# A gated convolution's input projection: one block group more, four plain column tiles fewer, operands taken unscaled

## The chip, the cores and the metric

One core of one Trainium2 chip. The metric is device time in microseconds (us), lower is better. The engines are TensorE (PE; its weight loads are PEld), VectorE (DVE), ScalarE (ACT), GpSimd (POOL) and SyncE (SP); SP and POOL mostly issue DMAs here.

## What is computed

A two-layer decoder trunk on x of 512 tokens by 1024 features: attention, a gated MLP, a short-convolution mixer, a gated MLP, each behind an RMS norm and added to the residual h. The change lies in the mixer:

```python
def short_conv_mixer(h, norm_g, w_in, conv_w, w_out):
    xn = rms_norm(h, norm_g)
    proj = xn @ w_in                      # 1024 -> 3072 columns
    gate_b, gate_c, u = proj[..., :1024], proj[..., 1024:2048], proj[..., 2048:]
    y = gate_b * causal_dwconv(gate_c * u, conv_w)   # width 3 along the tokens
    return y @ w_out
```

The norm is a gain per feature and one factor r per token (a row, since features lie on partitions and tokens along the free side). As r is a factor of each token, it can be applied to the input or to each projected column: `gate_c * u` then owes r twice, `gate_b` once.

## The kernel before, in words

All matrix products are in float32 split in two (high and low half, `whi`/`wlo` for weights, `hi`/`lo` for operands): three matmuls per product, high by high, high by low, low by high. ScalarE writes a high half, VectorE the low half (L1027 and L1029 in `halves_to`, L315 and L316 for plain weight tiles).

*Plain tiles.* A tile is 128 of the 3072 output columns: eight blocks of 128 input features, three matmuls of 512 tokens each, 24 matmuls (`products`, L336 to L338). They read `hs_a`/`hs_b`, halves of h times gain, unscaled by r, which the end of the first MLP writes (L372, L373). What comes out is multiplied by r.

*Block groups.* `Sevens` computes four tiles (two column tiles of one part by two of another) in seven products instead of eight: input features and tokens are cut in halves, and seven sums of quarters (forms p1, p7, p3, p6, p2, q5, q4) meet seven sums of weight blocks. A product is 24 matmuls of 256 tokens (`seven`, L1078); a group has 168. The forms are made once for all groups. The weight sums are made for each group: X and Y are loaded by SP (L1093, L1094), then Y += a block by a DMA of POOL (L1105), Y += X on VectorE (L1144), X += a block by a DMA of POOL (L1105), Y += W on VectorE (L1199); W and Z are loaded (L1102). Halves of each sum follow in `weights_of`. Halves of weights have three buffers, which plain tiles share. `slot(g, s)` writes out the order by hand: seven slots a group, each with its product (slot 2 has p3 of the group before) and the vector and scalar work around it.

The 24 column tiles of the mixer's projection are done as eight plain tiles (two of u, two of gate_c, the first four of gate_b) and four groups: groups 1 to 3 are two tiles of u and two of gate_c each, group 4 the last four tiles of gate_b. During the plain tiles the chore `prepare` makes x = h times gain times r (eight operations, L1453) and from it all seven forms (L1459, L1029), so that the groups' results need no r. `input_` (L1467, L1469, L446) does the two plain tiles of u and gate_c, `gate` (L1475) scales a tile of gate_b. `conv` is a scaled copy on ScalarE (L443) and two operations on VectorE (L446). `times` (L1404) multiplies by gate_b; group 4 does that in place. `halves_in` makes y's halves, which the out-projection (eight plain tiles, from 736.4 us) reads.

Order on an engine is the program's order as a scheduler with a cost model rearranges it, before the run; `pin` keeps an instruction in program order, `behind(a, b)` puts a behind b on its engine. Each engine and each DMA queue then takes its list in order.

Of the kernel before, what the change touches and what calls it, by code (L numbers as in the profile page):

```python
# [17 lines left out]
F32 = mybir.dt.float32  # L18
# [4 lines left out]
ALU = mybir.AluOpType  # L23
# [34 lines left out]
def trunk(  # L58
# [153 lines left out]
    def conv_tap(j, t):  # L212
        i = 24 + j * 8 + t
        return gains[:, i:i + 1]
# [51 lines left out]
    def want(dram, k0, nk, c0, n, *more):  # L266
        wanted.append((dram, k0, nk, (c0, n) + more))
# [173 lines left out]
    def causal_conv(dst, src, tap):  # L441

        act.activation(dst, src, AF.Copy, scale=tap(2))  # L443
        for j in (1, 0):
            d = 2 - j
            dve.scalar_tensor_tensor(dst[:, d:], src[:, 0:S - d], tap(j), dst[:, d:], op0=ALU.mult, op1=ALU.add)  # L446


    w_in, w_out = attn_w_in[0], attn_w_out[0]
# [36 lines left out]
    GROUPS = ((0, 2), (2, 2), (4, 2), (6, 1), (7, 2), (9, 2))  # L486

    def want_conv():
        for part, o in ((2, 0), (1, 0), (2, 1), (1, 1)) + tuple((0, o) for o in range(4)):
            want(conv_w_in[0], 0, 8, part * D + o * P, P)  # L490

    def want_conv_out():
        for o in range(ND):
# [532 lines left out]
    def halves_to(hi, lo, src, sign=1.0, held=()):  # L1026
        made = act.activation(hi, src, AF.Copy, scale=sign)  # L1027
        if sign > 0:
            rest = dve.tensor_tensor(lo, src, f32(hi), op=ALU.subtract)  # L1029
        else:  # L1030
            rest = dve.scalar_tensor_tensor(lo, src, -1.0, f32(hi), op0=ALU.mult, op1=ALU.subtract)
        for m, engine in ((made, "act"), (rest, "dve")):
            if engine in held:
                pin(m)

    LEFT, RIGHT = slice(0, HT), slice(HT, S)
    FORMS = ("p1", "p7", "p3", "p6", "p2", "q5", "q4")
# [45 lines left out]
    class Sevens:  # L1083
# [23 lines left out]
        def weights_of(self, g, form, n):  # L1107
            hi, lo = (wp.tile([P, CHUNK], F32R, tag=f"w{t}", name=f"w{t}_{form}{self.name}{g}", bufs=3)[:, 0:1024].rearrange(
                "p (k c) -> p k c", c=2 * P) for t in ("hi", "lo"))
            halves_to(hi, lo, self.st[g][n], held=("act",))  # L1110
            self.st[g][form] = hi, lo

        def bank_of(self, g, n):
# [16 lines left out]

        def join(self, g, n, acc, other):
            to = self.wides[g][n][:, :, RIGHT]
            dve.tensor_tensor(to, acc.rearrange("p (i t) -> p i t", t=HT), other.rearrange("p (i t) -> p i t", t=HT), op=ALU.subtract)
            if self.scaled:
                dve.tensor_tensor(to, to, self.row(RIGHT), op=ALU.mult)

# [4 lines left out]
        def first_sums(self, g):  # L1141
            self.weights_of(g, "p7", "Y")
            if not self.table:
                dve.tensor_tensor(self.st[g]["Y"], self.st[g]["Y"], self.st[g]["X"], op=ALU.add)  # L1144
            self.add_block(g, "X", 0, 1)
            if self.table:
                self.load_one(g, "three", self.table("6", g))
# [143 lines left out]
    class RawForms:  # L1291
# [9 lines left out]
        def make(self, name, k=slice(0, 4)):  # L1301
            (a, b), (c, d) = ((x[:, k, LEFT], x[:, k, RIGHT]) for x in self.x)
            s0, s1 = (t[:, k, :] for t in self.s)
            src, made = {
                "p1": (a, None), "p7": (s0, (a, b, ALU.subtract)), "p6": (s0, (s0, d, ALU.add)), "p2": (c, None),
                "q5": (s1, (b, d, ALU.subtract)), "q4": (d, None), "p3": (s0, (c, s0, ALU.subtract))}[name]
            if made:
                dve.tensor_tensor(src, made[0], made[1], op=made[2])
            halves_to(*(t[:, k, :] for t in self.up.forms[name]), src)

    def up_seven(layer, norm, mp):
        blocks, up = up_begin(layer, norm, mp, mp)
# [55 lines left out]
    def conv_seven(norm, mp, rp):  # L1368
# [2 lines left out]
            c0 = (4 + 2 * half) * P if g == 4 else (2 - half) * D + 2 * g * P  # L1371
            return conv_w_in[0][kh * 512:(kh + 1) * 512, c0:c0 + 2 * P].rearrange("(k p) c -> p k c", p=P)

        up = Sevens("c", mp, range(1, 5), block_of)
        up.norm, up.chores, up.ahead = norm, [], True
        chores, wides, room = up.chores, up.wides, []

        def eight(dt, name):
            t = rp.tile([P, 8, S], dt, tag="head", name=name)
            return t[:, 0:4, :], t[:, 4:8, :]  # L1380
        early_t, early_b = eight(F32, "early")
        ys = []

        def place(k, n):
            if not room:
                room.append(hsp.tile([P, 12, S], F32, tag="hs_a", name="hs_a_conv"))
            return room[0][:, k:k + n, :]
        up.wides_of = lambda g: {"yg": place(8, 2), "yv": place(10, 2)}

        def conv(o, src):  # L1390
            dst = early_t[:, 2 + o, :] if o < 2 else place(o, 1)[:, 0, :]
            causal_conv(dst, src, lambda i: conv_tap(i, o))

        def halves_in(o, n):
# [6 lines left out]

        def times(o, side, with_):
            t = place(o, 2)[:, :, side]
            dve.tensor_tensor(t, t, with_, op=ALU.mult)  # L1404

        def by_tile(acc):
            return acc.rearrange("p (i t) -> p i t", t=HT)
# [15 lines left out]
        def tail(p, s):  # L1423
            u, c = (wides[p][n] for n in ("yg", "yv"))
            if p == 4:
                if s == 0:
                    open_ys()
                    times(6, RIGHT, c[:, :, RIGHT])
                    times(4, RIGHT, u[:, :, RIGHT])
                    halves_in(4, 2)  # L1430
                elif s == 3:
                    halves_in(6, 2)
            elif s == 0:
                if p == 2:
                    halves_in(2, 2)
            elif s == 1:
                dve.tensor_tensor(u[:, :, RIGHT], u[:, :, RIGHT], c[:, :, RIGHT], op=ALU.mult)
            elif s in (3, 4):
                conv(2 * p + s - 3, u[:, s - 3, :])
            elif s == 5 and p == 1:  # L1440
                dve.tensor_tensor(place(0, 2), early_t[:, 2:4, :], early_b[:, 0:2, :], op=ALU.mult)
                times(2, slice(0, S), early_b[:, 2:4, :])
                open_ys()
            elif s == 6 and p == 1:
                halves_in(0, 2)
        up.tail = tail

        def prepare():
            x0, x1 = mp.tile([P, 4, S], F32, tag="x0", name="x0_prep"), rp.tile([P, 4, S], F32, tag="four", name="x1_prep")
            s0, s1 = (mp.tile([P, 4, HT], F32, tag=t, name=f"{t}_prep", bufs=2) for t in "XY")  # L1450
            for x, f in ((x0, 0), (x1, 4)):
                for i in range(4):
                    dve.scalar_tensor_tensor(x[:, i, :], h[:, f + i, :], gain_of(norm.base, f + i), norm.row, op0=ALU.mult, op1=ALU.mult)  # L1453
                    yield 0.75
            a, b, c, d = x0[:, :, LEFT], x0[:, :, RIGHT], x1[:, :, LEFT], x1[:, :, RIGHT]
            for n, src, made in (("p1", a, None), ("p7", s0, (a, b, ALU.subtract)), ("p6", s0, (s0, d, ALU.add)), ("p2", c, None),
                                 ("q5", s1, (b, d, ALU.subtract)), ("q4", d, None), ("p3", s0, (c, s0, ALU.subtract))):
                if made:
                    dve.tensor_tensor(src, made[0], made[1], op=made[2])  # L1459
                    yield 1.22  # L1460
                halves_to(*up.forms[n], src)
                yield 1.22

        def input_(o, u, c):
            x, y = early_t[:, 0, :], early_t[:, 1, :]
            for t, acc in ((x, u), (y, c)):
                dve.tensor_tensor(t, acc, norm.row, op=ALU.mult)  # L1467
                yield 0.69
            dve.tensor_tensor(x, x, y, op=ALU.mult)  # L1469
            yield 0.69  # L1470
            conv(o, x)
            yield 1.5

        def gate(o, acc):
            dve.tensor_tensor(early_b[:, o, :], acc, norm.row, op=ALU.mult)  # L1475
            yield 0.69

        accs = []
        for j in range(8):
            accs.append(bank("bbbbaabb"[j]))  # L1480
            for _ in products(accs[-1], weights(), (4, 5, 6, 7, 0, 1, 2, 3)):
                up.work_off(SHARE)
            if j in (1, 3):
                chores.append(input_(j // 2, *accs[j - 1:]))
            if j == 3:
                chores.append(prepare())
            if j >= 4:
                chores.insert(0, gate(j - 4, accs[j]))
            if j == 5:
                up.load_pair(1)  # L1490
                up.add_block(1, "Y", 1, 1)
            if j == 7:
                up.weights_of(1, "p1", "X")
                up.first_sums(1)
                up.weights_of(1, "p6", "Y")
        want_conv_out()
        for s in range(28):
            up.slot(1 + s // 7, s % 7)
            if s == 20:
                sum_far(99)  # L1500
            if s == 27:
                fetch(1)
        for s in (0, 2, 3):
            up.slot(5, s)
# [287 lines left out]
```

## Time and profile before

| | us |
|---|---|
| three runs | 1117.97, 1118.03, 1118.71 (median 1118.03) |
| profiled execution | 1119.06 |
| its span, first to last instruction | 1117.3 |
| plain tiles of the projection | 610.2 to 656.3 |
| four block groups | 656.3 to 736.4 |
| out-projection | 736.4 to 781.1 |

The granted TensorE clock is 1.00 of full speed in all stretches shown, its level of 2.4 GHz. An engine's busy time is the time in which it has an instruction under way; matmuls overlap, so a busy TensorE tells nothing of its rate, and a delay is read from the length of a run of equal matmuls.

### The profile page before, as it was taken

What the parts mean: (1) busy time and instruction counts of PE and PEld (TensorE: products, weight loads), DVE (VectorE), ACT (ScalarE), POOL (GpSimd) and SP (SyncE); (2) the same over time, 40 slices, a digit from 0 to 9 for tenths busy, and PEclk for the clock granted to TensorE, in tenths of its full rate; (3) what the DMA queues carried; (4) which work ended last, traced back from release to release, by engine and by line L of the source; (5) the groups of instructions that cost most, each with busy time, mean ns of one, the idle gap of its engine ahead of it and who ended that gap; (6) DMA issues with size and microseconds to landing.
All of it is one profiled execution on the core that took longest, in us unless ns stands there. A gap on an engine that the chain in (4) does not pass through costs nothing.

```text
span 1117.3 us, 19714 instructions
## 1 busy us (share of the span) xinstructions
PE 1109.9 (99%) x7803; PEld 1014.2 (91%) x7803; DVE 960.8 (86%) x1483; ACT 681.2 (61%) x1006; POOL 175.4 (16%) x199
## 2 busy tenths in 40 slices
PE   9999999999999999999999999999999999999998
PEld 7888787878899999999999899988999999998886
DVE  6798888997899787898989888867899999999886
ACT  7466677655466666666557355545666656567553
POOL 4011111111012221014400001110111221014300
PEclk9999999999999999999999999999999999999999
DMA  6668877778678887899963355696879887899951
GB/s 196 169 182 202 199 175 207 190 206 227 177 174 200 204 202 177 218 271 193 226 178 81 113 145 139 138 278 168 214 185 219 195 201 181 218 260 206 231 152 57
DMA packets 176988, 210.94 MB, mean 189 GB/s; under 512 B 7580, under 2 KB 142796, under 8 KB 176896
## 3 DMA queue, kind: packets, MB, share of 16 engines
q0 software_dynamic: 50112, 92.19, 42.7%
q1 hardware_dynamic: 126624, 117.42, 33.4%
q8 instruction: 61, 1.00, 0.3%
q14 instruction: 31, 0.25, 0.1%
q10 hardware_dynamic: 160, 0.07, 0.0%
HBM read 204.68 MB, written 44.04 MB: 223 GB/s over the span
## 4 chain that ended last, share of the span: by engine, by line
PE 96%; DVE 2%; issue 1%; ACT 1%; DVEq 0%; ACTq 0%
PE psb L1078 31%; PE psa L1078 12%; PE psb L1670 11%; PE psa L1670 8%; PE psb L336 6%; PE psb L338 5%; PE psb L337 5%; PE psb L710 2%; PE psa L338 2%; PE psa L337 2%; PE psa L336 2%; PE psa L807 2%; PE psc L782 1%; PE psb L592 1%; PE psb L593 1%; PE psb L594 1%
## 5 line engine op out<-in xcount | busy, mean ns | idle before, releaser
L1078 PE MATMUL psb<-p_hi,whi_p 128*128 128x256 f32 x480 | 135.4, 282 | 0.0
L1078 PE MATMUL psb<-p_lo,whi_p 128*128 128x256 f32 x480 | 135.2, 282 | 0.0
L1078 PE MATMUL psb<-p_hi,wlo_p 128*128 128x256 f32 x480 | 135.0, 282 | 0.0
L315 ACT ACTIVATE whi<-raw 128x1024 fp32r<-128x1024 f32 (+2 forms) x81 | 83.2, 1028 | 80.3 <-PE psb L337 27.8
L316 DVE TENSOR_TENSOR wlo<-raw,whi 128x1024 fp32r<-128x1024 f32 (+2 forms) x81 | 95.8, 1183 | 20.8 <-ACT whi L315 20.2
L1078 PEld LDWEIGHTS psb<-p_hi,whi_p 128*128 128x128 f32 x480 | 91.0, 189 | 0.0
L1078 PEld LDWEIGHTS psb<-p_lo,whi_p 128*128 128x128 f32 x480 | 90.5, 189 | 0.0
L1078 PE MATMUL psa<-p_hi,wlo_p 128*128 128x256 f32 x320 | 90.2, 282 | 0.0
L1078 PE MATMUL psa<-p_lo,whi_p 128*128 128x256 f32 x320 | 90.2, 282 | 0.0
L1078 PE MATMUL psb<-q_lo,whi_q 128*128 128x256 f32 x320 | 90.2, 282 | 0.0
L1078 PE MATMUL psb<-q_hi,whi_q 128*128 128x256 f32 x320 | 90.1, 282 | 0.0
L1078 PEld LDWEIGHTS psb<-p_hi,wlo_p 128*128 128x128 f32 x480 | 90.1, 188 | 0.0
L1078 PE MATMUL psa<-p_hi,whi_p 128*128 128x256 f32 x320 | 90.0, 281 | 0.0
L1078 PE MATMUL psb<-q_hi,wlo_q 128*128 128x256 f32 x320 | 90.0, 282 | 0.0
L336 PE MATMUL psb<-hs_a,whi 128*128 128x512 f32 x192 | 79.3, 413 | 0.0
L338 PE MATMUL psb<-hs_a,wlo 128*128 128x512 f32 x192 | 76.2, 398 | 0.0
L1670 PE MATMUL psb<-act,whi 128*128 128x256 f32 x352 | 63.3, 282 | 0.0
L1078 PEld LDWEIGHTS psa<-p_hi,whi_p 128*128 128x128 f32 x320 | 60.6, 190 | 0.1
L1078 PEld LDWEIGHTS psb<-q_hi,whi_q 128*128 128x128 f32 x320 | 60.6, 189 | 0.0
L1078 PEld LDWEIGHTS psa<-p_lo,whi_p 128*128 128x128 f32 x320 | 60.3, 189 | 0.1
L1078 PEld LDWEIGHTS psb<-q_lo,whi_q 128*128 128x128 f32 x320 | 60.4, 189 | 0.0
L1078 PEld LDWEIGHTS psa<-p_hi,wlo_p 128*128 128x128 f32 x320 | 60.1, 188 | 0.0
(551 smaller groups left out, 3596.7 us busy)
## 6 DMA issues: line engine op xcount, KB each, us to landing
t<-in_ffn_w_up POOLq DMA_DIRECT2D x24, 768.0 KB, 8.0
raw<-in_attn_w_in SPq DMA_DIRECT2D x24, 512.0 KB, 5.0
t<-in_ffn_w_up POOLq DMA_DIRECT2D x12, 1024.0 KB, 10.1
X<-in_ffn_w_up SPq DMA_DIRECT2D x20, 512.0 KB, 5.0
Y<-t SPq DMA_DIRECT2D x20, 512.0 KB, 6.6
three<-t SPq DMA_DIRECT2D x20, 512.0 KB, 5.4
W<-in_ffn_w_up SPq DMA_DIRECT2D x20, 512.0 KB, 4.0
Z<-in_ffn_w_up SPq DMA_DIRECT2D x20, 512.0 KB, 5.5
```

The lines of the kernel that those rows point to most:

```text
L315: return (act.activation(hi[:, at_], raw[:, at_], AF.Copy), dve.tensor_tensor(lo[:, at_], raw[:, at_], f32(hi[:, at_]), op=ALU.subtract))
L316: dve.tensor_tensor(lo[:, at_], raw[:, at_], f32(hi[:, at_]), op=ALU.subtract))
L336: made = [pe.matmul(acc, w[0], rhs[0], start=first, stop=False), pe.matmul(acc, w[0], rhs[1], start=False, stop=False), pe.matmul(acc, w[1 ...
L337: pe.matmul(acc, w[0], rhs[1], start=False, stop=False),
L338: pe.matmul(acc, w[1], rhs[0], start=False, stop=last)]
L592: pe.matmul(acc, lhs[0], w[0], start=first, stop=False)
L593: pe.matmul(acc, lhs[0], w[1], start=False, stop=False)
L594: pe.matmul(acc, lhs[1], w[0], start=False, stop=last)
L710: pe.matmul(ss[e][:, c:c + wide], ql[rows, b * P:n], kl[rows, 0:wide], start=first and b == bs[0], stop=last and b == bs[-1])
L807: pe.matmul(out_, w, t[:, first:first + step * (NB - k - 1) + 1:step, :], start=k == 0 and i == 0, stop=k == NB - 1 and i == 1)
L1078: pe.matmul(to, w[a][:, k, c], x[b][:, k, :], start=fresh and i + k + t == 0, stop=i == 1 and k == 3 and t == 2, skip_group_check=not fresh)
L1670: pe.matmul(to, l, r, start=begin and o + t == 0, stop=end and t == 2 and o == (0 if layer else 1), skip_group_check=not fresh)
```

## The change

Five groups and four plain tiles (the first four of gate_b). Group 0 takes the first two tiles of u and of gate_c. The forms are now sums of h times gain, without r, as the plain operands are: p1, p2 and q4 are plain quarters, which DMAs of POOL's queue copy from `hs_a`/`hs_b` (six copies, high and low half, 512 KB each); p7, p6, q5 and p3 are made by `RawForms` from eight copies on ScalarE (`raw.take`). So u times gate_c is multiplied by r squared (`row2`) in each of groups 0 to 3, and tiles 4 to 7 of the convolved product by r in two more products, since group 4's gate has no r either. Five vector operations are put behind others with `behind`: gate 3, q5's difference, p3's difference, the two products with r, and the convolution of tile 7 (six calls, the two products in one kind). The scratch of p7, p6 and q5 moves from X's and Y's buffers to `early`.

```diff
     def want_conv():
-        for part, o in ((2, 0), (1, 0), (2, 1), (1, 1)) + tuple((0, o) for o in range(4)):
-            want(conv_w_in[0], 0, 8, part * D + o * P, P)
+        for o in range(4):
+            want(conv_w_in[0], 0, 8, o * P, P)
...
-        up = Sevens("c", mp, range(1, 5), block_of)
+        up = Sevens("c", mp, range(5), block_of)
...
         def conv(o, src):
-            dst = early_t[:, 2 + o, :] if o < 2 else place(o, 1)[:, 0, :]
-            causal_conv(dst, src, lambda i: conv_tap(i, o))
+            return causal_conv(place(o, 1)[:, 0, :], src, lambda i: conv_tap(i, o))
...
             if p == 4:
                 if s == 0:
                     open_ys()
-                    times(6, RIGHT, c[:, :, RIGHT])
                     times(4, RIGHT, u[:, :, RIGHT])
                     halves_in(4, 2)
+                    behind(times(6, slice(0, S), both(norm.row)), up.joined)
+                    times(6, RIGHT, c[:, :, RIGHT])
...
             elif s == 1:
                 dve.tensor_tensor(u[:, :, RIGHT], u[:, :, RIGHT], c[:, :, RIGHT], op=ALU.mult)
+                if p == 3:
+                    behind(times(4, slice(0, S), both(norm.row)), up.rest)
             elif s in (3, 4):
-                conv(2 * p + s - 3, u[:, s - 3, :])
-            elif s == 5 and p == 1:
-                dve.tensor_tensor(place(0, 2), early_t[:, 2:4, :], early_b[:, 0:2, :], op=ALU.mult)
-                times(2, slice(0, S), early_b[:, 2:4, :])
-                open_ys()
+                if s == 3:
+                    dve.tensor_tensor(u, u, both(row2), op=ALU.mult)
+                if p < 3 or s == 3:
+                    conv(2 * p + s - 3, u[:, s - 3, :])
+            elif s == 5 and p < 2:
+                times(2 * p, slice(0, S), early_b[:, 2 * p:2 * p + 2, :])
+                if p == 1:
+                    open_ys()
...
+        def copied(name, k0, side):
+            for part, to in enumerate(up.forms[name]):
+                own_, at_ = (hs_now["b"], 0) if part and k0 else (hs_now["a"], 8 if part else k0)
+                pin(nc.gpsimd.dma_start(to, own_[:, at_:at_ + 4, side]))
...
+        def open_first():
+            up.load_pair(0)
+            copied("p1", 0, LEFT)
+            up.add_block(0, "Y", 1, 1)
+            copied("q4", 4, RIGHT)
+
+        copied("p2", 4, LEFT)
+        first = weights()
+        for f in (0, 1, 4, 5, 2, 3, 6, 7):
+            raw.take(f)
+        norm.scaled(lambda: dve.tensor_tensor(row2, norm.row, norm.row, op=ALU.mult))
+        accs = [bank("b") for _ in range(4)]
+        plan = {
+            (0, 7): open_first, (1, 0): lambda: (raw.make("p7"), up.weights_of(0, "p1", "X")), (1, 2): lambda: raw.make("p6"),
+            (2, 6): lambda: up.first_sums(0), (2, 7): lambda: (gate(0, accs[0]), gate(1, accs[1])), (3, 4): lambda: gate(2, accs[2])}
+        for j, acc in enumerate(accs):
+            for k, _ in enumerate(products(acc, weights() if j else first, (4, 5, 6, 7, 0, 1, 2, 3))):
+                if (j, k) in plan:
+                    plan[j, k]()
+        up.weights_of(0, "p6", "Y")
         want_conv_out()
-        for s in range(28):
-            up.slot(1 + s // 7, s % 7)
-            if s == 20:
+        for s in range(35):
+            up.slot(s // 7, s % 7)
+            if s == 0:
+                behind(gate(3, accs[3]), up.rest)
+                behind(raw.make("q5"), up.summed)
+            if s == 2:
+                behind(raw.make("p3"), up.rest)
+            if s == 27:
                 sum_far(99)
-            if s == 27:
+            if s == 34:
+                behind(conv(7, wides[3]["yg"][:, 1, :])[0], up.joined)
                 fetch(1)
```

Removed with it, not shown: `prepare` and `input_`, and the loop over eight plain tiles that fed chores between matmuls. `up.rest` is the low half that `weights_of` made last, `up.summed` Y plus X of `first_sums`, `up.joined` the difference that `join` made last.

## Rows read from the trace of the kernel before

**Rows 1.** The page: span, and the chain that ended last by engine.
```profile
span 1117.3 us, 19714 instructions
...
PE 96%; DVE 2%; issue 1%; ACT 1%; DVEq 0%; ACTq 0%
```

**Rows 2.** Stretches: length, busy us by engine (instructions), clock, DMA share, GB/s; VectorE alone.
```profile
610.20:633.96 23.76, 23.76 (x109) 19.16 (x109) 20.34 (x38) 10.57 (x15) 0.00 (x0) 1.00 0.46 133
633.96:656.28 22.32, 22.32 (x99) 18.10 (x98) 21.91 (x24) 10.31 (x11) 0.00 (x0) 1.00 0.28 87
656.28:673.56 17.28, 17.28 (x146) 17.12 (x146) 14.66 (x14) 9.37 (x12) 2.59 (x2) 1.00 0.78 192
673.56:693.45 19.89, 19.89 (x171) 19.89 (x170) 16.82 (x19) 12.34 (x16) 2.58 (x2) 1.00 0.68 160
693.45:713.74 20.29, 20.29 (x170) 20.01 (x170) 17.06 (x19) 10.41 (x14) 2.58 (x2) 1.00 0.50 105
713.74:736.45 22.71, 22.71 (x194) 22.71 (x193) 20.54 (x24) 12.15 (x14) 4.15 (x5) 1.00 0.82 194
811.80:1000.00 188.20, 188.20 (x1586) 188.20 (x1585) 177.35 (x225) 117.50 (x145) 31.84 (x26) 1.00 0.83 205
...
sum 126.25, DVE 111.33; mean DVE 18.55
```

**Rows 3.** VectorE's timeline: start, duration, line, out<-in, [idle before <-releaser], q5's low halves.
```profile
683.94 1.23 DVE L1029 TENSOR_TENSOR wlo_q5c<-Xc,whi_q5c 128x1024 fp32r<-128x1024 f32 x1 [1.13 <-ACT whi_q5c L1027]
...
705.80 1.23 DVE L1029 TENSOR_TENSOR wlo_q5c<-Xc,whi_q5c 128x1024 fp32r<-128x1024 f32 x1 [2.61 <-ACT whi_q5c L1027]
...
723.88 1.23 DVE L1029 TENSOR_TENSOR wlo_q5c<-Xc,whi_q5c 128x1024 fp32r<-128x1024 f32 x1 [0.89 <-ACT whi_q5c L1027]
```

**Rows 4.** VectorE's timeline: the last low half of the plain operands.
```profile
617.43 0.74 DVE L373 SCALAR_TENSOR_TENSOR hs_a<-h,gains,hs_a 128x512 fp32r<-128x512 f32 x1
```

**Rows 5.** DMA issues (600 to 740, then whole run), and L1105's time to landing, 600 to 780.
```profile
Xc<-in_conv_w_in POOLq DMA_DIRECT2D x4, 512.0 KB, 6.9
...
Yc<-in_conv_w_in POOLq DMA_DIRECT2D x3, 512.0 KB, 9.7
...
raw<-in_ffn_w_down POOLq DMA_DIRECT2D x4, 512.0 KB, 5.4
...
head_blocks<-head_blocks POOLq DMA_DIRECT2D x6, 256.0 KB, 7.4
...
Y_chain<-in_ffn_w_down POOLq DMA_DIRECT2D x2, 512.0 KB, 16.1
...
DMA to landing us min/median/max: 5.7/7.5/10.1
```

**Rows 6.** ScalarE's timeline, 613 to 623: idle before.
```profile
615.14 0.72 ACT L372 ACTIVATE hs_a<-h,gains 128x512 fp32r<-128x512 f32 x1 [1.84 <-DVE h L1606]
...
619.13 1.06 ACT L315 ACTIVATE whi<-raw 128x1024 fp32r<-128x1024 f32 x1 [1.60 <-PE psb L337]
...
622.34 1.06 ACT L315 ACTIVATE whi<-raw 128x1024 fp32r<-128x1024 f32 x1 [2.16 <-PE psb L337]
```

**Rows 7.** VectorE's groups by form, 610 to 741: busy us, mean ns, idle before.
```profile
L1453 DVE SCALAR_TENSOR_TENSOR x_prep<-h,gains,nrow_n 128x512 f32<-128x512 f32 x8 | 6.0, 746 | 0.0
...
L1029 DVE TENSOR_TENSOR p_loc<-x_prep,p_hic 128x1024 fp32r<-128x1024 f32 x2 | 2.4, 1218 | 0.0
...
L1467 DVE TENSOR_TENSOR early<-psb,nrow_n 128x512 f32<-128x512 f32 x4 | 2.7, 687 | 1.5 <-ACT nrow_n L397 1.4 <-PE psb L338 0.2
```

**Rows 8.** The border to the out-projection: VectorE's timeline of y's low halves, and TensorE's chain.
```profile
736.19 1.23 DVE L1029 TENSOR_TENSOR y_lo<-hs_a_conv,y_hi 128x1024 fp32r<-128x1024 f32 x1
...
739.14 1.23 DVE L1029 TENSOR_TENSOR y_lo<-hs_a_conv,y_hi 128x1024 fp32r<-128x1024 f32 x1
...
739.24 0.23 PE psa L336
...
744.81 0.23 PE psa L336
```

More of the change, by code (lines that the diff above doesn't have):

```diff
@@ L443, in causal_conv @@
         act.activation(dst, src, AF.Copy, scale=tap(2))
+        made = []
         for j in (1, 0):
             d = 2 - j
-            dve.scalar_tensor_tensor(dst[:, d:], src[:, 0:S - d], tap(j), dst[:, d:], op0=ALU.mult, op1=ALU.add)
+            made.append(dve.scalar_tensor_tensor(dst[:, d:], src[:, 0:S - d], tap(j), dst[:, d:], op0=ALU.mult, op1=ALU.add))
+        return made
     w_in, w_out = attn_w_in[0], attn_w_out[0]
@@ L1034, in halves_to @@
                 pin(m)
+        return rest
     LEFT, RIGHT = slice(0, HT), slice(HT, S)
@@ L1109, in weights_of @@
                 "p (k c) -> p k c", c=2 * P) for t in ("hi", "lo"))
-            halves_to(hi, lo, self.st[g][n], held=("act",))
+            self.rest = halves_to(hi, lo, self.st[g][n], held=("act",))
             self.st[g][form] = hi, lo
@@ L1132, in join @@
             to = self.wides[g][n][:, :, RIGHT]
-            dve.tensor_tensor(to, acc.rearrange("p (i t) -> p i t", t=HT), other.rearrange("p (i t) -> p i t", t=HT), op=ALU.subtract)
+            self.joined = dve.tensor_tensor(
+                to, acc.rearrange("p (i t) -> p i t", t=HT), other.rearrange("p (i t) -> p i t", t=HT), op=ALU.subtract)
             if self.scaled:
@@ L1143, in first_sums @@
             if not self.table:
-                dve.tensor_tensor(self.st[g]["Y"], self.st[g]["Y"], self.st[g]["X"], op=ALU.add)
+                self.summed = dve.tensor_tensor(self.st[g]["Y"], self.st[g]["Y"], self.st[g]["X"], op=ALU.add)
             self.add_block(g, "X", 0, 1)
@@ L1306, in make @@
                 "q5": (s1, (b, d, ALU.subtract)), "q4": (d, None), "p3": (s0, (c, s0, ALU.subtract))}[name]
-            if made:
-                dve.tensor_tensor(src, made[0], made[1], op=made[2])
+            made = made and dve.tensor_tensor(src, made[0], made[1], op=made[2])
             halves_to(*(t[:, k, :] for t in self.up.forms[name]), src)
+            return made
     def up_seven(layer, norm, mp):
@@ L1381, in conv_seven @@
         early_t, early_b = eight(F32, "early")
+        row2 = mp.tile([P, S], F32, tag="row2", name="row2")
         ys = []
@@ L1403, in times, with both @@
             t = place(o, 2)[:, :, side]
-            dve.tensor_tensor(t, t, with_, op=ALU.mult)
+            return dve.tensor_tensor(t, t, with_, op=ALU.mult)
+        def both(t):
+            return t[:, None, :].to_broadcast([P, 2, S])
         def by_tile(acc):
@@ L1446, in conv_seven @@
         up.tail = tail
[L1448 to L1472, printed above, removed]
-        def gate(o, acc):
[L1475 to L1495, printed above, removed]
@@ L1496, in conv_seven @@
-        want_conv_out()
-        for s in range(28):
-            up.slot(1 + s // 7, s % 7)
-            if s == 20:
+        x0, x1 = mp.tile([P, 4, S], F32, tag="x0", name="x0_raw"), rp.tile([P, 4, S], F32, tag="four", name="x1_raw")
+        raw = RawForms(up, (x0, x1), *(early_t[:, k:k + 2, :].rearrange("p i (j t) -> p (i j) t", t=HT) for k in (0, 2)))
+        def copied(name, k0, side):
+            for part, to in enumerate(up.forms[name]):
+                own_, at_ = (hs_now["b"], 0) if part and k0 else (hs_now["a"], 8 if part else k0)
+                pin(nc.gpsimd.dma_start(to, own_[:, at_:at_ + 4, side]))
@@ new lines, in gate @@
+        def gate(o, acc):
+            return dve.tensor_tensor(early_b[:, o, :], acc, norm.row, op=ALU.mult)
+        def open_first():
[9 more added lines that the diff above has]
+        accs = [bank("b") for _ in range(4)]
```

## The prediction

> **What bounds the kernel now.** I read the page first: the chain that ended last is 96% TensorE [rows 1]. So a change is worth what it takes out of, or puts into, TensorE's stream, and work elsewhere counts only where TensorE waits for it. Next the table of stretches, cut at the borders of the convolution's input projection [rows 2]. TensorE is busy through every stretch; a stall inside one shows as length beyond that of an undisturbed one. One block group takes 19.89 us (673.56 to 693.45, no stall). The group after it takes 20.29, so 0.40 is lost there. The stretch 656.28 to 673.56 is group 1 without its third product, six of seven products: 17.28 against 6/7 of 19.89, 17.05, so 0.23 is lost. Where the 0.40 goes, the vector engine's timeline shows: it sat idle 2.61 us for the high half of q5's weights [rows 3], which come behind an accumulating DMA into X. VectorE has the least room of the other engines: 111.33 us of the 126.25 from 610.20 to 736.45, 88% [rows 2].
>
> The profiled execution took 1119.06 us, 1.76 of it around its span of 1117.3 [rows 1], and lies 1.03 above the median of 1118.03. I work the difference out on its clock and take it off the median.
>
> **TensorE: what goes and comes.** The last four of the eight plain tiles fill 633.96 to 656.28, 22.32 us for 96 matmuls of 512 columns [rows 2]. They go (which four is the same: each has 24). In their place comes a fifth group, 168 matmuls of 256 columns, 19.89. Difference: -2.43 us. By columns alone it would be 7/8, -2.79; the short matmuls give 0.36 back. The norm's matmuls and transposes stay.
>
> **When group 0 needs what.** It starts where four tiles end, at 633.96, one product each 2.84: p1 at 633.96, p7 at 636.8, p6 at 639.6, p2 at 642.5, q5 at 645.3, q4 at 648.2. The cover over the preparation of operands shrinks from 46 us to 24. That is where the change can lose.
>
> *Forms by copy (p1, p2, q4).* Six DMAs of 512 KB on POOL's queue, where POOL before was at 0.00 in both stretches [rows 2]. The last low half of the operands is done at 618.17 [rows 4], so p1's pair is issued from about 618 on, with the accumulation into Y pinned behind it and q4's pair behind that; p2's go earlier, near 609. No row has a copy from SBUF to SBUF that rounds. Bounds: 5.4 us to landing (a plain copy from POOL's queue) and 16.1 (the slowest kind on that queue); an SBUF to SBUF accumulation of half the size took 7.4 [rows 5]. I take 7.4 to 10: p1 lies there by 628 to 629, 5 us before its use. Cost zero; the two ends are priced in the rivals.
>
> *The chain into q5*, the longest: Y's accumulation issued about 618.9, 9.7 to land [rows 5]: 628.6. Halves of p7's weights, 1.06 + 1.22, Y plus X, 1.22: 632.1. X's accumulation, 6.9 [rows 5]: 639.0. Halves of q5's weights, 2.3: 641.3. Due 645.3, so 4 us are over. p7's weights, ready at 630.9, have 5.9. Each landing may slip.
>
> *Forms from raw values.* Eight scaled copies on ScalarE at 0.72 = 5.8 us (price: the same form of copy, with a gain); its idle stretches after 613 alone give 1.84 + 1.60 + 2.16 [rows 6], and scaling by the norm no longer stands before any form. Cost zero; were that cover gone, one such copy ahead of an operand's last high half would delay it, and at worst TensorE, by 0.72.
>
> *VectorE.* Goes: the six scalings and products of the two early tiles at 0.69, four low weight halves at 1.22, eight scaled inputs at 0.75, three low halves of forms at 1.22 [rows 7]: 4.1 + 4.9 + 6.0 + 3.7 = 18.7. Comes: nine 1.22 operations of group 0's weights, four of 0.69 of its outputs, the squared row 0.69, four products with it at 1.22, two products with the plain row at 1.22: 11.0 + 2.8 + 0.7 + 4.9 + 2.4 = 21.8. Net +3.1, so 114.4 of 123.8 us, 92%. In the second MLP the same seven-product pattern ran at 177.35 of 188.20, 94%, with TensorE hardly delayed: its 66 products at 19.89 / 7 are 187.5, so at most 0.7 was lost in 188 [rows 2]. So 92% alone costs nothing. The 1.22 per group falls in the conv part of a slot, where VectorE idled 1.13, 2.61 and 0.89 us ahead of q5's low half [rows 3].
>
> *The ties.* Each only orders an operation on VectorE behind another there; they move gate 3, q5's and p3's forms, two products with the row and tile 7's convolution out of the way of weights. Behind them wait: group 1's T and R banks (gate 3 is done by about 638, those are due past 651), q5's form (about 641, due 645.3), p3 (due past 656). Zero.
>
> *The tail.* Two more products of 1.22 stand ahead of y tiles 4 and 5, three ahead of 6 and 7. The first low half ends at 737.42 and is read at 739.24, 1.8 over; the second at 740.37, read at 744.81, 4.4 over [rows 8]. VectorE idled 2.17 in the stretch before [rows 2]. So 2.44 against 4.0, 3.66 against 6.6: zero, but with 0 to 1 us as bounds.
>
> **Sum.** -2.43 on TensorE. The 0.63 of old stalls may vanish, and as much may come at the new border; I let them cancel: 1118.03 - 2.43 = **1115.6 us**. A measurement of this kernel can tell about 0.2%, 2.24 us, from no change: the forecast is just beyond that.
>
> **A rule against it.** POOL's DMA instructions of this stage landed in 5.7 to 10.1 us while VectorE was 85% busy [rows 2, 5]. The Trainium skill, "SBUF — State Buffer", "SBUF: two separate sides", says that a DMA from GpSimd's queue can stand still, because its descriptors can't be written while VectorE runs an operation in a two-port mode. The kind it names is a float32 copy, and the long operations here all have two sources; if it held for them, the copies would crawl and the time would be that of the third rival. By that rule 0.02 of that rival's chance.
>
> **Rivals.**
> (1) *The gain is eaten by small stalls.* VectorE at 92% runs late at the few places with a deadline: the four q5 chains, of which one had no room before, and p7 and y. For it: 0.23 and 0.40 lost at 86%. Against: the second MLP. Five groups losing 0.4 more each, and 0.5 at the border, are +2.5: 1118.1, no change. It runs from 1116.1 to 1120.3. Chance 0.26.
> (2) *The old stalls go too*, since less stands ahead of X's accumulation: -2.43 - 0.63 = -3.06, 1115.0. Chance 0.12.
> (3) *Slower: the copies hold up POOL's queue.* Mechanism: Y's and X's accumulations stand in one queue with six copies; with a landing of L us each, q5's weights are ready at 618.9 + L + 3.5 + L + 2.3 = 624.7 + 2L, due 645.3. Free until L = 10.3. At L = 12.7 the stall is 4.7, which turns the gain into a loss beyond 0.2%. At 16.1, the slowest row [rows 5], it is 11.6: 1115.6 + 11.6 = 1127.2. For it: two such DMAs issued together already take 9.7 for the second, and here five stand together. Against: the 16 DMA engines are 46% and 28% busy there [rows 2], and plain copies took 5.4. Chance 0.10.
> (4) *The change doesn't do what it says*: the form copies or the order put the first group before its inputs, and TensorE idles just that 2.4: as before, 1118.0; counted in (1).
>
> **How the numbers follow.** The forecast has 0.52, rival (2) 0.12, (1) 0.26, (3) 0.10. The forecast's own spread is 1115.2 to 1116.3 (tail 0 to 1, border 0 to 0.7, old stalls 0 to -0.63); some 0.4 of its 0.52 lies under 1115.8. Faster: 0.40 + 0.12 = 0.52. Same: 0.12 + 0.26 = 0.38. Slower: 0.10. The range for 8 in 10 takes in the forecast, (2), and the larger part of (1): 1114.8 to 1118.3.
>
> **What would show it.** Right: one stretch of four plain tiles of 5.6 us and 35 block products of 2.84, the first near 634, and out-projection starting near 734; the DVE row near 92% of that stretch; copies landing before 629. Rival (1): products longer than 2.85 ahead of q5, p7 or at 734, released by VectorE. Rival (3): TensorE idle at p1 or q5 of group 0, behind ScalarE waiting for a DMA into X or a form. The forecast is wrong if the stage from 610.2 to the out-projection is not 123 to 125 us long, or if the time outside it moves by over 0.5 us.

## The result, and the profile after

The changed kernel takes 1121.29 us (median of 11 runs, 1120.61 to 1123.27); the kernel before, run beside it, 1118.83 (median of 11 runs; ten of them lie between 1117.95 and 1120.69, and one slow run of 2180.49 is not in the ratio). Ratio 1.0021, 95% interval 1.0012 to 1.0031: slower by 2.5 us, some 0.2%, where 2.4 less was forecast. The page has a span 1.6 us longer than [rows 1]. Its chain can be followed back only to 636.42 us, 43% of the span, so its 38% of TensorE are not to be set beside the 96% there; the other engines and DMAs hold some 5 of the 43:

```profile
span 1118.9 us, 19900 instructions
...
PE 38%; issue 2%; DVE 2%; DMA 1%; ACT 0%; DVEq 0%; ACTq 0%; POOLq 0%
```

The whole loss lies in one stretch: from the first matmul of the first plain tile to the first product of the second MLP. I call its length D. Before it is 610.02 to 780.94, 170.92 us; after it is 609.12 to 782.54, 173.42: 2.50 more, against 2.46 between the medians. After D both profiles have the same 336.3 us left. Ahead of it the same instructions ended up to 3.4 us apart among the profiled runs told of below (the first plain tile begins between 608.55 and 611.95), so I compare D and its parts, not single totals.

Table of stretches of the kernel after (columns as in [rows 2]): four plain tiles; group 0 (six products); groups 1, 2 and 3; group 4 with the last p3 (eight products); the output projection. Then, of the kernel before, the output projection:

```profile
609.12:632.87 23.75, 23.75 (x110) 19.26 (x109) 19.95 (x34) 16.10 (x24) 4.48 (x6) 1.00 1.14 285
632.87:651.99 19.12, 18.17 (x146) 17.34 (x144) 16.98 (x18) 10.21 (x12) 2.62 (x2) 1.00 0.62 138
651.99:671.92 19.93, 19.93 (x170) 19.93 (x169) 17.74 (x19) 10.51 (x13) 2.60 (x2) 1.00 0.68 160
671.92:691.88 19.96, 19.96 (x170) 19.96 (x169) 18.19 (x20) 11.87 (x15) 2.59 (x2) 1.00 0.68 159
691.88:711.84 19.96, 19.96 (x170) 19.96 (x169) 17.75 (x20) 10.78 (x14) 2.59 (x2) 1.00 0.51 106
711.84:736.30 24.46, 23.30 (x195) 22.89 (x193) 20.81 (x24) 11.04 (x14) 4.06 (x5) 1.00 0.73 175
736.30:782.54 46.24, 45.06 (x194) 35.88 (x193) 31.89 (x40) 24.05 (x35) 3.17 (x5) 1.00 0.84 215
```
```profile
736.29:780.94 44.65, 44.65 (x195) 36.05 (x194) 28.49 (x36) 22.84 (x34) 3.21 (x5) 1.00 0.86 221
```

The clock column stays at 1.00. Groups 1 to 3 cost what an undisturbed group cost before (19.89, [rows 2]), 0.18 more in all, and both old stalls are gone. The loss sits at three places: group 0 took 19.12 where six products are 17.05, so 2.07 lost; group 4 and the last p3 24.46 where eight products are 22.73, so 1.73; the output projection 1.59 more than before. Sum: -2.43 - 0.63 (old stalls) + 2.07 + 0.18 + 1.73 + 1.59 = 2.51.

TensorE's timeline, cut to the rows with idle time, says who released it at each place:

```profile
642.02 0.38 PE L1081 MATMUL psa<-p_hic,wlo_p2c 128*128 128x256 f32 x1 [0.21 <-DVE wlo_p2c L1031]
...
645.20 0.39 PE L1081 MATMUL psb<-q_hic,whi_q5c 128*128 128x256 f32 x1 [0.30 <-ACT whi_q5c L1029]
646.15 0.38 PE L1081 MATMUL psb<-q_hic,whi_q4c 128*128 128x256 f32 x1 [0.44 <-ACT whi_q4c L1029]
...
712.42 0.39 PE L1081 MATMUL psa<-p_hic,wlo_p1c 128*128 128x256 f32 x1 [0.17 <-DVE wlo_p1c L1031]
...
730.73 0.39 PE L1081 MATMUL psb<-q_hic,wlo_q4c 128*128 128x256 f32 x1 [0.99 <-DVE wlo_q4c L1031]
...
741.52 0.50 PE L337 MATMUL psa<-y_lo,whi 128*128 128x512 f32 x1 [1.18 <-DVE y_lo L1031]
```

The bracketed idle time is less than the loss, since a matmul is shown as busy for 0.28 us while the next starts 0.12 after it. So I use the length of a product from its first matmul to that of the next (2.85 undisturbed): 3.78 for p2 of group 0, 6.79 for its q5 and q4 together, 3.29 for p1 of group 4, 4.11 for its q4.

*Group 0.* ScalarE's timeline, then VectorE's:

```profile
631.05 1.06 ACT L1029 ACTIVATE whi_p7c<-Yc 128x1024 fp32r<-128x1024 f32 x1 [2.27 <-DMA Yc<-in_conv_w_in]
...
643.14 1.06 ACT L1029 ACTIVATE p_hic<-early 128x1024 fp32r<-128x1024 f32 x1 [0.86 <-DVE early L1311]
644.11 1.04 ACT L1029 ACTIVATE whi_q5c<-Xc 128x1024 fp32r<-128x1024 f32 x1
645.05 1.04 ACT L1029 ACTIVATE whi_q4c<-Yc 128x1024 fp32r<-128x1024 f32 x1
```
```profile
640.75 1.22 DVE L1031 TENSOR_TENSOR wlo_p2c<-Wc,whi_p2c 128x1024 fp32r<-128x1024 f32 x1
641.89 1.22 DVE L1311 TENSOR_TENSOR early<-x_raw,early 128x1024 f32<-128x1024 f32 x1
644.23 1.23 DVE L1031 TENSOR_TENSOR p_loc<-early,p_hic 128x1024 fp32r<-128x1024 f32 x1 [1.13 <-ACT p_hic L1029]
645.37 1.22 DVE L1031 TENSOR_TENSOR wlo_q5c<-Xc,whi_q5c 128x1024 fp32r<-128x1024 f32 x1
```

Two things are late. The halves of p7's weights wait for Y, and p3's form (L1311, with its halves) stands on both engines ahead of q5's weights, though p3 is not multiplied before 657.67. p7's own product still took 2.86; but from its low half at 632.14 to 643.11 VectorE works without a break, and so the lateness reaches p2's low half and the form behind it. The DMA issues of 605 to 636, with the time to landing:

```profile
p_loc<-hs_a POOLq DMA_DIRECT2D x1, 512.0 KB, 8.5
Yc<-in_conv_w_in POOLq DMA_DIRECT2D x1, 512.0 KB, 11.9
q_hic<-hs_a POOLq DMA_DIRECT2D x1, 512.0 KB, 12.7
...
Xc<-in_conv_w_in POOLq DMA_DIRECT2D x1, 512.0 KB, 5.7
```

Y's accumulation took 11.9 us. The DMA share of the first stretch, 1.14 at 285 GB/s, is more than double the 0.46 and 133 that the same stretch had before [rows 2].

*Group 4.* VectorE's timeline, then ScalarE's:

```profile
724.86 1.23 DVE L1031 TENSOR_TENSOR wlo_q5c<-Xc,whi_q5c 128x1024 fp32r<-128x1024 f32 x1 [2.72 <-ACT whi_q5c L1029]
726.00 1.22 DVE L1450 TENSOR_TENSOR hs_a_conv<-hs_a_conv,row 128x1024 f32<-128x1024 f32 x1
...
729.46 1.22 DVE L1031 TENSOR_TENSOR wlo_q4c<-Yc,whi_q4c 128x1024 fp32r<-128x1024 f32 x1
```
```profile
727.25 0.72 ACT L443 ACTIVATE hs_a_conv<-hs_a_conv,gains 128x512 f32<-128x512 f32 x1 [1.94 <-DVE hs_a_conv L1450]
727.88 1.05 ACT L1029 ACTIVATE whi_q4c<-Yc 128x1024 fp32r<-128x1024 f32 x1
```

VectorE idles 2.72 us (the idle of [rows 3]) and only then makes the product with the squared row. ScalarE's first step of the convolution waits for that product, and q4's weights queue behind the convolution.

*Border.* VectorE's, then ScalarE's timeline, to set beside [rows 8]:

```profile
736.18 1.21 DVE L1408 TENSOR_TENSOR hs_a_conv<-hs_a_conv,nrow_n 128x1024 f32<-128x1024 f32 x1
...
740.25 1.21 DVE L1031 TENSOR_TENSOR y_lo<-hs_a_conv,y_hi 128x1024 fp32r<-128x1024 f32 x1
```
```profile
736.84 1.06 ACT L315 ACTIVATE whi<-raw 128x1024 fp32r<-128x1024 f32 x1 [2.24 <-DMA raw<-in_conv_w_out]
738.03 1.06 ACT L1029 ACTIVATE y_hi<-hs_a_conv 128x1024 fp32r<-128x1024 f32 x1
```

The first low half of y, at 736.19 before, is at 740.25. A product for tiles 6 and 7 stands ahead of the one for tiles 4 and 5, and on ScalarE a weight half that waits for a DMA stands ahead of y's high half.

### The profile page after: what moved, and what is told of

Read it like the earlier page. It is cut to its first block, busy times and chain, and to the rows that moved or that the text cites. A ratio compares the mean times of both kernels' runs of the same rounds, so it can differ in the third digit from the quotient of the medians.

```text
span 1118.9 us, 19900 instructions
## 1 busy us (share of the span) xinstructions
PE 1108.0 (99%) x7875; PEld 1014.9 (91%) x7875; DVE 964.0 (86%) x1482; ACT 687.9 (61%) x1018; POOL 182.5 (16%) x207
## 5 line engine op out<-in xcount | busy, mean ns | idle before, releaser
L315 ACT ACTIVATE whi<-raw 128x1024 fp32r<-128x1024 f32 (+2 forms) x77 | 79.0, 1027 | 70.9 <-PE psb L337 22.2
L316 DVE TENSOR_TENSOR wlo<-raw,whi 128x1024 fp32r<-128x1024 f32 (+2 forms) x77 | 90.8, 1180 | 19.9 <-ACT whi L315 19.5
L336 PE MATMUL psb<-hs_a,whi 128*128 128x512 f32 x176 | 72.7, 415 | 0.0
L338 PE MATMUL psb<-hs_a,wlo 128*128 128x512 f32 x176 | 70.0, 398 | 0.0
```

Of the source, the lines that this page charges most:

```text
L315: return (act.activation(hi[:, at_], raw[:, at_], AF.Copy), dve.tensor_tensor(lo[:, at_], raw[:, at_], f32(hi[:, at_]), op=ALU.subtract))
L316: dve.tensor_tensor(lo[:, at_], raw[:, at_], f32(hi[:, at_]), op=ALU.subtract))
L336: made = [pe.matmul(acc, w[0], rhs[0], start=first, stop=False), pe.matmul(acc, w[0], rhs[1], start=False, stop=False), pe.matmul(acc, w[1 ...
L338: pe.matmul(acc, w[1], rhs[0], start=False, stop=last)]
```

## The experiments

Three theories. *Order*: a few operations stand at the wrong place in VectorE's or ScalarE's list, and moving them, with no work removed, gives the time back. *Amount*: VectorE has some 3 us too much to do, and any order stalls. *Copies*: the form copies hold up the accumulations on POOL's queue. D and its two parts (to the first and from the first matmul of the output projection), one profile each. Places that an edit does not touch differ by up to 0.6 us between these runs (p1 of group 4 took 3.29 in the run of after and 3.88 in e2), so a smaller difference in D is read only together with the products in which it lies:

```
                         to output  output   D       D - after
before                   126.27     44.65    170.92  -2.50
after                    127.18     46.24    173.42
e1 squared row early     125.17     48.52    173.69  +0.27
e2 p3's form later       126.15     46.26    172.41  -1.01
e3 q4's copies first     128.62     46.25    174.87  +1.45
e4 tiles 6, 7 later      126.68     45.15    171.83  -1.59
e6 Y's sum first         126.63     46.27    172.90  -0.52
e7 no ties               126.70     45.66    172.36  -1.06
e11 q4's copies late     127.11     46.27    173.38  -0.04
e9 e1+e2+e4+e6+ACT tie   123.83     45.27    169.10  -4.32
e12 e9 without ACT tie   124.26     47.62    171.88  -1.54
e10 e9 + 4 products      125.89     44.77    170.66  -2.76
```

**e1: the product with the squared row, early.**

```diff
@@ early
                 dve.tensor_tensor(u, u, by_tile(acc), op=ALU.mult)
+                w = wides[g]["yg"]
+                squared[g] = dve.tensor_tensor(w, w, both(row2), op=ALU.mult)
+        squared = {}
@@ tail, s == 3
-                    dve.tensor_tensor(u, u, both(row2), op=ALU.mult)
+                    behind(up.rest, squared[p])
```

> The product of u with the squared row is put ahead of the low half of q5's weights on VectorE, so that it fills the idle time there (2.72 us in group 4 of the changed kernel, 1.12 in group 3); same work, other order. Theory 'order' (the stalls come from where a few operations stand in the lists of VectorE and ScalarE): the slot of q4 in group 4 falls from 4.11 us to under 3.1, and p1 of group 4 from 3.29 to about 2.9; the stretch of block groups is 1.4 to 1.8 us shorter. Theory 'amount' (VectorE simply has 3 us too much work): both slots stay within 0.3 us. Theory 'copies' (POOL's queue is late): both stay, since no copy is under way there.

Both lengthened products of group 4 fell to 2.84, which is 1.72 less, with the same work on VectorE. The part ahead of the output projection is 2.01 shorter; the rest is p2 of group 0, 3.38 instead of 3.78, which the edit does not touch (see e6). But the gain was lost at the border. ScalarE's timeline there:

```profile
736.90 1.06 ACT L315 ACTIVATE whi<-raw 128x1024 fp32r<-128x1024 f32 x1 [4.40 <-DMA raw<-in_conv_w_out]
737.86 1.99 ACT L1029 ACTIVATE y_hi<-hs_a_conv 128x1024 fp32r<-128x1024 f32 x2
```

The output projection begins 2.09 earlier than in the run of after, but that weight half starts at 736.90, as late as then (736.84), and y's high halves queue behind it. Its transfer was issued 2.43 us earlier (730.01, not 732.44) and took 6.8 us instead of 4.3.

**e2: p3's form two slots later.**

```diff
-            if s == 2:
+            if s == 4:
                 behind(raw.make("p3"), up.rest)
```

> p3's form of group 0 is made behind q4's weights instead of behind p2's; it is needed only 15 us later. Theory 'order': q5's and q4's weights no longer wait behind it on ScalarE and VectorE; the slots of q5 and q4 of group 0 together fall from 6.79 us to about 5.9, total 0.8 to 1.2 us less. Theory 'copies': X's accumulation lands too late whatever stands behind it: the two slots stay within 0.3 us. Theory 'amount': the 2.3 us of work move elsewhere, as does the stall.

q5 and q4 together fell from 6.79 to 5.70, no loss at all, and p2 to 3.30: the end of p2's 3.78 had been the wait for q5. Group 0 took 17.60 instead of 19.12, so the place of p3's form costs 1.52 of its 2.07. p1 of group 4 went up to 3.88, though the edit does not touch it, and so D is only 1.01 shorter.

**e3: q4's copies issued early.**

```diff
@@ open_first
             up.add_block(0, "Y", 1, 1)
-            copied("q4", 4, RIGHT)
@@ before the plain tiles
         copied("p2", 4, LEFT)
+        copied("q4", 4, RIGHT)
```

> q4's two copies are issued next to p2's, near 608, ahead of p1's, instead of behind the accumulation into Y. Theory 'copies': the accumulation into Y, issued at 619.1 and landed by 631.0 in the changed kernel (11.9 us), lands 1.5 to 4 us sooner, X's accumulation is issued as much sooner, and group 0's stall of 2.0 us falls under 0.8. Theory 'order': Y lands sooner, but q5's weights still stand behind p3's form: the stall of group 0 falls by less than 0.6. Theory 'amount': no change beyond 0.3.

It went the other way from what every theory had: p7 of group 0 took 4.39, D is 1.45 longer. The issues of 605 to 636:

```profile
p_loc<-hs_a POOLq DMA_DIRECT2D x1, 512.0 KB, 11.0
Yc<-in_conv_w_in POOLq DMA_DIRECT2D x1, 512.0 KB, 13.9
```

Copies that lie behind Y in the queue do no harm; put in front, they do.

**e4: the product of y tiles 6 and 7 behind the low half of 4 and 5.** (The helpers also return their instruction.)

```diff
-                    halves_in(4, 2)
-                    behind(times(6, slice(0, S), both(norm.row)), up.joined)
+                    behind(times(6, slice(0, S), both(norm.row)), halves_in(4, 2))
```

> The product of y tiles 6 and 7 with the row is put behind the low half of y tiles 4 and 5, instead of behind a join ahead of it. Theory 'order': the first out-projection tiles no longer wait 1.2 to 1.5 us for y's low half; from the first plain tile to the second MLP 45.0 to 45.4 us instead of 46.4. Theory 'amount': the wait moves to y tiles 6 and 7, and the stretch stays above 46.

The output projection took 45.15, 1.09 less, as 'order' had it; the rest of the 1.59 in D lies in group 4 and group 0, where its q4 and p2 came out at 3.88 and 3.45 though nothing there was edited.

**e6: group 0's Y summed ahead of the copies.**

```diff
@@ open_first
-            up.load_pair(0)
             copied("p1", 0, LEFT)
-            up.add_block(0, "Y", 1, 1)
             copied("q4", 4, RIGHT)
@@ before the plain tiles
+        up.load_pair(0)
+        up.add_block(0, "Y", 1, 1)
         copied("p2", 4, LEFT)
```

> Edit: group 0's pair of loads and the accumulation into Y are issued ahead of the first form copy on POOL's queue, so Y no longer moves in the crowded 610 to 631. 'Landing' theory (group 0's second to sixth products wait for Y's late landing, 11.9 us in the run of after): Y lies there by about 605, p7's weights are ready well ahead, X's accumulation is issued some 5 us earlier, the p2 slot falls from 3.78 to at most 3.3 and the pair q5 and q4 from 6.79 towards 5.7 to 6.2; total 1.0 to 1.6 us under the changed kernel. 'Order' theory alone (p3's form ahead of q5's weights decides): Y's place changes nothing in the pair q5 and q4, since the form still stands ahead of them; it stays at 6.6 to 6.8, total at most 0.5 less. 'Amount' theory: no change, as the vector engine's work is the same. Groups 3 and 4 and the border stay at 3.3, 4.1 and 12.7 in all theories.

Issues of 590 to 609:

```profile
Yc<-in_conv_w_in POOLq DMA_DIRECT2D x1, 512.0 KB, 5.9
```

Alone on the DMA engines, the sum that took 11.9 us took 5.9. p2 fell to 3.37; q5 and q4 stayed at 6.78 although X's accumulation is issued 2.1 us earlier from the first plain tile (24.40 after it, not 26.53). So Y's lateness is worth the 0.41 of p2, and the rest is as 'order' had it: q5 waits for p3's form. Runs that leave Y's sum where it was agree. Counted from the first plain tile, p7's high half, which waits for Y, began after 21.93, 21.72, 21.59 and 21.43 us in the runs of after, e11, e4 and e1; p2 took 3.78, 3.60, 3.44 and 3.38.

**e7: without the ties**, that is with `behind(...)` taken off gate 3, q5's and p3's forms, the two products with the row and tile 7's convolution.

> Edit: the change without its five ties and the tie of gate 3 (nothing else differs). The prediction put them at zero. 'Ties do harm in group 0' ('order' theory): without them q5's and p3's forms stand early on the vector engine, among the small operations of the norm, and not ahead of q5's weights: pair q5 and q4 back at 5.7 to 5.9 (from 6.79), q4 of group 4 at 3.0 to 3.5 (the product with the squared row stands ahead of q5's low half again); but the row of the norm comes later by the 4.9 us of the forms, so gate 0 to 3 and the fourth bank are later, which may cost up to 1.5 at the first products of group 0; border: the first y high half stands ahead of the third weight tile, 11.2 to 12.0 instead of 12.74. Total 1.0 to 2.5 us under the changed kernel. 'Ties pay': their absence costs 1 to 4 us, by products of group 0 or 4 that wait for weights behind moved operations. 'Amount' theory: total within 0.3 of the changed kernel, the stalls only change places.

D is 1.06 shorter: together the ties cost time. The losses change place. The forms now stand among the small operations of the norm, gates and p7's weights come late (p6 of group 0: 3.97), and p1 of group 4 takes 3.86; q4 of group 4 is back at 2.83, since the scheduler now puts the product with the squared row ahead of q5's low half there (721.81, before 724.85), as e1 does by hand. q5 and q4 of group 0 came to 6.35, not to the 5.7 to 5.9 expected.

**e11: q4's copies issued after X's accumulation.**

```diff
@@ open_first
-            copied("q4", 4, RIGHT)
@@ plan
-            (2, 6): lambda: up.first_sums(0),
+            (2, 6): lambda: (up.first_sums(0), copied("q4", 4, RIGHT)),
```

> Edit: of the changed kernel, the two copies of q4's form are issued behind X's accumulation on POOL's queue (due only at the seventh product) and not right behind Y's. 'Engines full' theory (Y's accumulation lands late because the 16 DMA engines are shared with q4's copies and the loads of group 1 that run beside it): with 1 MB less beside it Y lands 2 to 4 us earlier than the 11.9 us after its issue, that is in 8 to 10 us; the first four slots of group 0 come to 11.4 to 11.7 instead of 12.3 (the p2 slot 3.2 to 3.4 instead of 3.78). The pair q5 and q4 stays at 6.6 to 6.8, since p3's form still stands ahead of q5's weights, unless q4's copies now land after 648, when it grows. 'Queue' theory (an accumulation from POOL's queue is slow by itself there): Y lands in 11 to 12.5 us as before and the p2 slot stays at 3.7 to 3.8. All other places as in the changed kernel; from the first plain tile to the second MLP's first product 172.6 to 173.0 by the first, 173.3 to 173.5 by the second (173.42 in the run of after).

Issues of 605 to 636:

```profile
Yc<-in_conv_w_in POOLq DMA_DIRECT2D x1, 512.0 KB, 11.7
```

D is the same within 0.04, and Y landed as late, so what stands behind Y is not what delays it. (p2 took 3.60, a little less than the 3.7 to 3.8 that 'queue' had.) Over the runs Y's sum took 5.9 us alone, 11.4 to 11.9 behind p1's two copies, 13.9 with q4's in front too, the latter two while loads of SP's queue were under way. How much of it is the place in POOL's queue and how much the loads, these runs do not separate.

**e9: five places at once.** e1, e2, e4 and e6, and the third output weight tile's high half tied on ScalarE (the two lists hold that weight half and the last high half of y):

```diff
@@ end of conv_seven
+        y_high = high_last[0]; fetch(1 + AHEAD); behind(made_last[0], y_high)
         return ys, place
```

> Edit: five places at once, no work removed: the product with the squared row early in each group (as in e1), p3's form behind q4's low half (e2), the tile 6 and 7 product with the row behind the low half of y tiles 4 and 5 (e4), group 0's Y accumulation ahead of the copies (e6), and the third output weight tile's high half on ScalarE behind the high half of y tiles 6 and 7. The vector engine does as much as in the changed kernel, 92% or more of the stage. 'Order' theory: with each operation in an idle place the stalls of the changed kernel (5.3 us: 0.93 + 1.09 in group 0, 0.44 + 1.26 in group 4, 1.57 at the border) fall to under 1.5, total 3.8 to 5 under the changed kernel, 1115.5 to 1117 on the record's scale, that is 1 to 2.5 under the kernel before. 'Amount' theory: VectorE at 92% keeps TensorE waiting somewhere whatever the order; at least 3 of the 5.3 us stay, total not under 1118.5 and no faster than before.

1116.6 us (10 runs, 1115.85 to 1120.58) against 1119.19 (13 runs): ratio 0.9979, 95% interval 0.9967 to 0.9991, some 0.2% faster than the kernel before, while the changed kernel is 0.2% slower than it. Its table of stretches, group 0, group 4 and output projection:

```profile
634.33:651.50 17.17, 17.17 (x146) 17.16 (x144) 14.47 (x15) 10.31 (x12) 2.64 (x2) 1.00 0.70 154
...
711.37:734.41 23.04, 23.00 (x195) 22.80 (x193) 21.23 (x24) 11.02 (x14) 2.85 (x3) 1.00 0.72 170
734.41:779.68 45.27, 44.92 (x194) 35.97 (x193) 31.14 (x40) 23.47 (x34) 4.09 (x6) 1.00 0.88 228
```

Over D VectorE is busy 143.46 us, as in the changed kernel (143.31). Up to the output projection its share is even higher, 112.33 of 123.83 us, 90.7%, against 111.42 of 127.18, 87.6%. The work is the same, and 2.07, 1.73 and 1.59 have shrunk to 0.12, 0.31 and 0.62. 'Amount' falls as the cause of these stalls.

**e12: e9 without its tie on ScalarE.**

> Edit: the combination of e9 without its tie on ScalarE, so that the high half of the third output weight tile stands again ahead of the high halves of y tiles 4 to 7. 'Place' theory: that weight half waits for its transfer, which landed at 736.9 in the run of e1, whatever comes before; y's high halves queue behind it though their data is ready near 735.6. The first two output tiles take 2 to 4 us longer than the combination's, from the start of the out-projection to the second MLP's first product 47 to 48.6 (combination 45.27), and all of the stage before stays within 0.2 of 123.83. 'Amount' theory: the tie on ScalarE changes no work and so nothing; 45.0 to 45.5.

ScalarE's timeline at the border:

```profile
736.91 1.06 ACT L315 ACTIVATE whi<-raw 128x1024 fp32r<-128x1024 f32 x1 [4.81 <-DMA raw<-in_conv_w_out]
737.88 1.04 ACT L1029 ACTIVATE y_hi<-hs_a_conv 128x1024 fp32r<-128x1024 f32 x1
```

The output projection took 47.62: one weight half at the wrong place costs 2.35. The stretch ahead is 0.43 longer than in e9, more than the 0.2 expected; p1 of group 4 took 3.55 (3.15 in e9).

**e10: e9 with the product of the squared row made twice.**

> Edit: the combination of e9 with the product of the gated input and the squared row made twice in each of groups 0 to 3, one right behind the other: 4 x 1.22 = 4.9 us more on the vector engine, and an output in which that factor stands once too often. The combination had VectorE busy for 112.33 of 123.83 us from the first plain tile to the out-projection (90.7%); this has 117.2 of about 124 (94 to 95%). 'Amount' theory: the vector engine's load sets the stalls, so the whole stage falls back: 3 to 5 us longer than the combination's 123.83. 'Order' theory: the added operation stands in the same idle place, so each group loses at most what exceeds the idle left there (idle 11.5 us over the stage, 2.3 a group): 0 to 1.5 us longer, 123.8 to 125.3.

The stretch up to the output projection, then group 2 and group 3 in it:

```profile
609.43:735.32 125.89, 124.83 (x951) 119.28 (x949) 117.10 (x134) 70.40 (x90) 17.01 (x18) 1.00 0.73 171
```
```profile
670.25:690.24 19.99, 19.99 (x171) 19.96 (x169) 19.20 (x21) 10.27 (x14) 2.58 (x2) 1.00 0.69 159
690.24:711.35 21.11, 20.64 (x171) 20.03 (x169) 19.59 (x22) 11.55 (x16) 2.58 (x2) 1.00 0.49 100
```

4 x 1.22 = 4.9 us more on VectorE lengthened this part by 2.06, above the 1.5 that 'order' allowed and under the 3 of 'amount', and D by 1.56, as the output projection, where nothing was edited, came out 0.50 shorter than in e9. The 2.06 lie in group 3 (21.11, in e9 19.96) and group 4 with the last p3 (23.97, in e9 23.04), behind a group 2 in which VectorE was busy for 19.20 of 19.99 us. So load counts too, once a group leaves hardly any idle time; of the added work more than half still cost nothing. One run at one place gives no limit for the share.

## Why the prediction was wrong

Three steps that the sum put at nothing failed: p3's form ahead of q5's weights (1.52 us by e2), the product with the squared row that was to fall in idle time (1.7 by e1), and the tail (1.59). In each the work was counted, but not what stands behind it in the engine's list.

- *TensorE, -2.43.* Right: a fifth group at the old groups' length in place of four tiles. With the stalls mostly removed (e9) D is 1.82 under before.
- *Copies cost zero.* Right for what they feed: p1 of group 0 ran in 2.83 as soon as the tiles ended. Wrong for their neighbours. "The 16 DMA engines are 46% and 28% busy there" was taken from the kernel before, though the copies and group 0's and group 1's loads were themselves what fills that stretch. Rival (3) had the place and the mechanism; by e6 its price is 0.4, not the 4.7 (4.8 by its own formula) to 11.6 worked out for it. That the copies alone make Y late is not shown, since the loads ran beside them.
- *The rule against it.* The copies did not crawl: with VectorE busy for 19.95 of 23.75 us, the form copies ahead of Y landed within 8.5. The rule, in the Trainium skill, "SBUF — State Buffer", "SBUF: two separate sides", speaks of operations in a two-port mode and names a float32 copy. VectorE's long operations in that stretch all have two sources, so these runs do not test the rule.
- *The chain into q5, "4 us are over".* Y's landing took 11.9, not 9.7, and a gate stands between Y's operations. X still lay there at 641.35 (635.65 plus 5.7), with q5 due 2.85 after p2's start at 641.42, at 644.27, so the 2.3 for q5's halves just fitted. What used the room up was p3's form, on which the prediction said "p3 (due past 656). Zero". It asked whether p3 itself would be late, not who queues behind its form. e2 shows 1.5 us there.
- *VectorE +3.1, "falls in the conv part of a slot".* The amount was right over D: 143.31 against 139.84, 3.5 more. The share was not: up to the output projection VectorE was busy for 111.42 of 127.18 us, 88% where 92% was forecast, because the stalls pushed the rest behind the border (31.89 us in the output projection, 28.49 before). Nor was the place: in groups 3 and 4 the product stands behind q5's low half, the idle time ahead of that half passes unused, and weights behind it come late. e1, which moves just that product, took 1.7 off p1 and q4 of group 4.
- *The ties, zero.* Wrong: 1.06 together (e7), as a net sum, for without them other places lose.
- *The tail, zero with 0 to 1 as bounds.* It cost 1.59, beyond the bound. The sum counted operations ahead of each y tile, not their order, and left out ScalarE's list, where a weight half that waits for a DMA stands ahead of y's high half. e4 takes 1.09 off; e12 against e9 shows 2.35 for the ScalarE place once the rest comes earlier.
- *Old stalls cancel the new border.* The old ones went, as rival (2) had it; the new ones were 5.57 in all, 1.59 of them at the border, not 0.63.

The outcome was of the kind of rival (1), small stalls, but they came to 2.07 + 0.18 + 1.73 + 1.59 = 5.57 where it had 2.5, and for another reason: not VectorE's load, but four or five operations in the wrong place.

One thing varies between kernels that do not touch it: p1 and q4 of group 4, by a few tenths. The traces tie this to the landing of the accumulation into X. ScalarE's timeline of the runs of after and e2, q5's high half in group 3:

```profile
702.21 1.06 ACT L1029 ACTIVATE whi_q5c<-Xc 128x1024 fp32r<-128x1024 f32 x1 [2.88 <-DMA Xc<-in_conv_w_in]
```
```profile
702.62 1.06 ACT L1029 ACTIVATE whi_q5c<-Xc 128x1024 fp32r<-128x1024 f32 x1 [3.50 <-DMA Xc<-in_conv_w_in]
```

Counted from the start of group 3 these are 10.33 and 10.94 us, and 10.48 in e6, 10.78 in e11; p1 of group 4 took 3.29, 3.89, 3.45 and 3.72. What moves the landing is open.

## What to carry to other kernels

When a change adds operations to an engine that runs in order, ask of each one what stands behind it in the list, not only how long it takes and whether its own result is due late. Idle time in front of an instruction covers new work only if the new work stands in front of it. And an engine's load before the change does not bound the traffic in a stretch that the change itself fills.

## What the runs showed that was not expected

A step that comes earlier can be worth nothing, or less, if the head of the next list waits for a transfer that does not land earlier: in e1 the output projection could begin 2.09 us earlier, ScalarE waited 4.40 us for a weight transfer, and D grew by 0.27. And the same accumulating transfer of 512 KB took 5.9 us alone and 13.9 behind other copies in its queue and beside loads of another, so that one landing time is no property of a kind of DMA.
